# Order of the high and low parts in split float32 products, with an opening and an addition re-placed

## The chip, the cores and the metric

The kernel runs on one core of one Trainium2 chip. The metric is the device time of one execution in microseconds (us). TensorE (PE) multiplies matrices into PSUM, VectorE (DVE) and ScalarE (ACT) do the elementwise work, and transfers are issued from queues of SyncE (SP), ScalarE and GpSimd (POOL).

## The reference

One residual block of a streaming encoder on x of 2048 tokens by 1024 channels, all in float32:

```python
h = rmsnorm(x, norm_mix_pre)
proj = h @ w_in                      # 1024 -> pool 512 | glu 2*512 | gate_a 1024 | gate_b 1024
branch_a = pool_mixer(u_pool, pool_w, pool_scale, w_pool_out)
branch_b = conformer_conv(u_glu, conv_w, conv_b, ln_g, ln_b, w_conv_out)   # glu, width-31 causal conv, layernorm, silu
merged = sigmoid(g_a) * branch_a + sigmoid(g_b) * branch_b
x = x + rmsnorm(merged @ w_o, norm_mix_post)
h = rmsnorm(x, norm_mlp_pre)
f = square(relu(h @ w_up)) @ w_down   # 1024 -> 4096 -> 1024
x = x + rmsnorm(f, norm_mlp_post)
```

## The kernel before, in words

**Split operands.** TensorE gets each float32 operand as two reduced-precision parts: a high part, which ACT makes with a cast (lines 230 and 237), and a low part, which is the operand minus its high part and is made by DVE (line 131, in `split` and `split_w`). A product of operands a and b is hi*hi + hi*lo + lo*hi. So a weight tile is the pair `wh`, `wl`, and a token tile, called a cell, is a pair of tiles in the buffers `big`, `tr` or `fo`. A cell is 128 partitions by 1024: two slices of 128 channels, each for 512 tokens (`T`). Two cells make the 512-deep contraction of one product.

**One product.** `product` (line 301) multiplies one weight tile by two cells into a PSUM tile of 1024 columns, two halves q = 0 and 1. It has 24 matmuls of 128x512: for each half q, four slices k of the contraction (k = 0, 1 from the first cell, 2, 3 from the second), each with the three pairs of parts. `matmuls` (line 276) does the half q = 0 in full and then q = 1. The order within a half is that of `passes` (line 271): for k = 0, 1, 2 weight-high with cell-high and with cell-low; then the low weights of k = 0, 1, 2; then the three of k = 3. So the first cell's low part is read by the second matmul, the second cell's by the sixth, the low weights by the seventh. Calls that go straight to `matmuls` (the products named A, B, and wo of the first block of tokens) use the same order.

In the opening `product` hands over to `in_order` (line 312), which walks a list of (q, k, weight part, cell part). `STAIRS` (line 59) goes through one cell after the other, per cell high*high, then weight-high with cell-low, then weight-low with cell-high, four matmuls each, two for each half. `in_order` can also call a function when it has come to a given matmul (`inside`), so that what the function issues is placed there in the queues.

**Fast matrix multiplication.** Most of the products are those of a Strassen-like scheme with seven products for eight, numbered 1 to 7. An `Octet` (line 461) holds one such group: weights and cells are single tiles or sums and differences of tiles (`weight_parts`, line 339, `token_parts`), and three PSUM accumulators x, z, y take products 1, 6, 7, 4, then 2, then 5, 3. After each product `Octet.run` copies the accumulator out (`held`, line 475) or calls a `sink`, which adds a held copy to PSUM with DVE (`add`, line 128) and goes on. The accumulator can't be written by its next product before that.

**Stages.** w_in is used in groups glu, pool, ga and gb, for the first block of 1024 tokens, then for the second; then A, B and wo; then up (eight octets a block) and down. Beside the matmuls DVE runs the width-31 convolution (lines 1066 and 1070) as background work, in lanes that a call to `bg` after each product moves on by some instructions.

**Order of work.** A planner puts the program's instructions in each engine's queue from its own costs, by a priority that is the place in the program. `tc.high_priority(offset=n)` moves that priority n instructions forward; `URGENT` is 1500, `ahead[0]` is 45 at first and 260 later. `behind` puts background work after the marked instructions of the main line. Each queue runs in order. In the opening (`opening`, from line 1673 on) the order of DVE, ACT, PE and SP is instead written out: `fix`, an `InOrder`, ties each instruction to the one traced before it.

**The opening.** Its products 1 to 4 are glu of the octet o1, on tokens 0 to 511, products 5 and 6 are `o2.run(1)` and `o2.run(2)`. The next products come from `run_first` (line 603): four of o1 on tokens 512 to 1023 (products 7 to 10), then o2's 5, 6, 3, 7. Products 7 and 8 need the cells 8 and 3, made of x in tokens 512 to 1023. For these x is scaled by a gain per channel (`first_gain`, two ACT instructions of line 852) and by the root of the norm per token (a DVE product, line 134), with the root spread over partitions by PE (`n1.spread`, line 771) and copied to `r` by ACT (line 914). Before, this work is traced after product 5 (up to cell 8) and after product 6 (cell 3), `first_cell` (line 924) scales the cells.

Of the kernel before, what the change touches and what calls it, by code (L numbers as in the profile page):

```python
# [57 lines left out]
ORDER = (1, 2, 6, 5, 7, 3, 4)  # L58
STAIRS = tuple(
    (q, 2 * c + k, wp, xp)  # L60
    for c in (0, 1) for wp, xp in ((0, 0), (0, 1), (1, 0)) for q in (0, 1) for k in (0, 1)
)
COMING = tuple((q, k, 0, 0) for k in (0, 1) for q in (0, 1)) + ((0, 0, 0, 1), (1, 0, 0, 1))
# [13 lines left out]
def block_kernel(  # L77
# [49 lines left out]
    def add(o, a, b):  # L127
        return nc.vector.tensor_tensor(o, a, b, op=ALU.add)  # L128
# [21 lines left out]
    def mark(i):  # L150
        marks[i.ins.engine] = i.ins
        return i
# [147 lines left out]

    def product(ps, w, cells, start=True, stop=True):

        if in_opening:
            in_order(STAIRS, ps, w, cells, start, stop)
            return
        rhs = cell_rhs(cells)
        i = [matmuls(half_of(ps, q), w, 4 * q, rhs, start, stop) for q in (0, 1)]
        mark(i[1])

    in_opening = [True]  # L310

# [149 lines left out]
    class Octet:  # L461
# [18 lines left out]

        def run(self, i, then, bg):
            w, cells = self.w.pop(i, None) or self.weight(i), self.parts.need(i)
# [6 lines left out]
            ps = self.ps[acc]  # L489
            product(ps, w, cells, start=begins, stop=i in (2, 3, 4))  # L490
            flush()
# [27 lines left out]
    class Plain:  # L519
# [57 lines left out]
        def run(self, job, then, bg, inside=(None, None)):  # L577
# [7 lines left out]
            if t == 0:  # L585
                order = COMING if (m, k) == (0, 0) else STAIRS
                in_order(order, self.ps, w, cells, k == 0, k == 1, inside)
            else:
                product(self.ps, w, cells, start=k == 0, stop=k == 1)
            flush()  # L590
# [12 lines left out]
    def run_first(o, p, bg, dve):  # L603

        jobs = [(o, (m, 1, k)) for m in (0, 1) for k in (0, 1)]
        jobs += [(p, i) for i in (5, 6, 3, 7, 4)]
        for n, (u, i) in enumerate(jobs[:-1]):
            v, j = jobs[min(n + LOOK[n], len(jobs) - 1)]
            u.run(i, v.part(j) if v is o else j, bg)
            if n in NORM:  # L610
                dve.skip()
                o.norm(NORM.index(n))
                dve()
# [310 lines left out]
    def first_cell(c, t):  # L924
        x = x0[c, t]
        if t or c > 1:
            first_gain(c, t)
            mul(two(x), two(x), per_token(r0[t]))
            return x
# [624 lines left out]
    def mlp_up(b, parts):  # L1554
        def one(u):
# [117 lines left out]
    def opening():  # L1673
# [50 lines left out]
        with tc.high_priority(offset=URGENT):  # L1724
# [18 lines left out]
        fix()  # L1743
        o2.run(2, None, none)
        with tc.high_priority(offset=URGENT):
            o1.prepare(0, 1, 1)
            cells0(2, 1), cells0(3, 1)
            parts.need(3)
            o1.cast_behind = [
                i for i in nc.cur_bb.bb.instructions if i.engine == mybir.EngineType.Activation  # L1750
            ][-1]
        fix()
        o1.load_behind = fix.last[E.SP]
        dve.last.update(fix.last)
        in_opening.clear()

# [800 lines left out]
```

## Time and profile before

| | us |
|---|---|
| Median of 3 runs | 2153.82 (2153.32 to 2154.16) |
| The profiled execution | 2153.48 |
| Its span on the core | 2151.7 |
| TensorE busy | 2130.3 (99%) |
| VectorE busy | 1653.8 (77%) |
| ScalarE busy | 1047.7 (49%) |

A row of a timeline has the start, the length of the row, engine and line, the operation, its output and input by the program's names, the shapes and a count; a bracket is the idle time of the engine just before the row, with what ended it. Matmuls overlap in the pipeline, so the pace is read from starts and not from the length of one. A row of the view of windows has, per engine, busy us and number of instructions, and at the end the granted TensorE clock, the share of DMA and GB/s.

### The profile page before, as it was taken

The numbers are of one execution on the slowest core, as the hardware profiler recorded it, in microseconds if no ns is written. First come the engines' busy times: TensorE is split into PE (matmuls) and PEld (weight loads), VectorE is DVE, ScalarE is ACT, GpSimd is POOL, SyncE is SP. The second block draws the span as 40 slices with busy tenths as digits, with TensorE's granted clock in tenths as the row PEclk, the third lists the DMA queues.
The fourth block names the chain that finished last, engine by engine and source line by source line (L and its number), as shares of the span: only waits on it lengthen the run. The fifth ranks groups of instructions, "written<-read, shape, count | busy, mean of one in ns | idle before, by whom it ended". The sixth has DMA issues, their size and how long they took to land.

```text
span 2151.7 us, 25228 instructions
## 1 busy us (share of the span) xinstructions
PE 2130.3 (99%) x9549; PEld 1764.8 (82%) x9549; DVE 1653.8 (77%) x1621; ACT 1047.7 (49%) x1123; POOL 78.4 (4%) x143
## 2 busy tenths in 40 slices
PE   9999999999999999999999999999999999999998
PEld 7888888888888887888888888888888888888887
DVE  7898589997778869997868795667776657576975
ACT  8445454334443635445554684645663332234751
POOL 1000000000000000000000000000000000120002
PEclk9999999999999999999999999999999999999999
DMA  8789897768897787445697698677898997996977
GB/s 309 250 301 344 310 354 263 270 246 304 338 362 251 267 320 270 169 148 200 248 352 296 244 347 319 249 262 277 316 347 313 346 379 258 336 366 236 302 260 209
DMA packets 174506, 620.49 MB, mean 288 GB/s; under 512 B 19504, under 2 KB 21808, under 8 KB 174384
## 3 DMA queue, kind: packets, MB, share of 16 engines
q1 hardware_dynamic: 143456, 508.01, 64.8%
q0 software_dynamic: 17824, 64.07, 8.4%
q10 hardware_dynamic: 13104, 46.80, 5.5%
q8 instruction: 75, 1.23, 0.2%
q14 instruction: 47, 0.39, 0.0%
HBM read 408.99 MB, written 209.81 MB: 288 GB/s over the span
## 4 chain that ended last, share of the span: by engine, by line
PE 90%; DVE 5%; DMA 3%; ACT 1%; issue 1%; SPq 0%; DVEq 0%; ACTq 0%
PE up L280 24%; PE down L280 22%; PE wo L280 8%; PE ga L280 7%; PE gb L280 7%; PE glu L280 5%; PE rb L280 5%; PE A L280 4%; PE B L280 4%; PE pool L280 3%; DVE y L1070 1%; DVE big L131 1%; DVE tr L131 1%; PE glu L319 1%; DVE wl L131 1%
## 5 line engine op out<-in xcount | busy, mean ns | idle before, releaser
L280 PE MATMUL up<-big,wh 128*128 128x512 f32 x1792 | 481.3, 390 | 5.0 <-DVE tr L128 4.2
L280 PEld LDWEIGHTS up<-big,wh 128*128 128x128 f32 x1792 | 336.4, 188 | 76.2 <-issue 3.9
L237 ACT CAST wh<-wr 128x1024 fp32r<-128x1024 f32 x196 | 205.8, 1051 | 336.2 <-PE up L280 101.8
L1070 DVE SCALAR_TENSOR_TENSOR y<-v,cst,y 128x1024 f32<-128x1024 f32 x240 | 307.5, 1281 | 3.1
L280 PE MATMUL down<-big,wh 128*128 128x512 f32 x872 | 294.9, 389 | 0.0
L237 ACT CAST wh<-ws 128x1024 fp32r<-128x1024 f32 x128 | 134.6, 1052 | 302.3 <-PE up L280 91.6
L280 PE MATMUL up<-big,wl 128*128 128x512 f32 x896 | 277.0, 390 | 0.0
L280 PE MATMUL down<-big,wl 128*128 128x512 f32 x688 | 212.0, 389 | 0.0
L131 DVE TENSOR_TENSOR wl<-ws,wh 128x1024 fp32r<-128x1024 f32 x120 | 146.5, 1221 | 76.1 <-ACT wh L237 75.6
L280 PEld LDWEIGHTS up<-big,wl 128*128 128x128 f32 x896 | 168.7, 188 | 35.0
L280 PE MATMUL down<-tr,wh 128*128 128x512 f32 x504 | 196.2, 389 | 0.5 <-DVE tr L131 0.5
L280 PEld LDWEIGHTS down<-big,wh 128*128 128x128 f32 x872 | 163.6, 188 | 33.9
L131 DVE TENSOR_TENSOR wl<-wr,wh 128x1024 fp32r<-128x1024 f32 (+1 forms) x121 | 146.3, 1211 | 32.3 <-ACT wh L237 32.3
L131 DVE TENSOR_TENSOR big<-big,big 128x1024 fp32r<-128x1024 f32 (+1 forms) x108 | 129.9, 1221 | 41.0 <-ACT big L1205 19.6
L131 DVE TENSOR_TENSOR tr<-tr,big 128x1024 fp32r<-128x1024 f32 x94 | 112.6, 1221 | 56.5 <-ACT big L1975 43.8
L280 PEld LDWEIGHTS down<-big,wl 128*128 128x128 f32 x688 | 129.1, 188 | 26.8
L280 PE MATMUL wo<-big,wh 128*128 128x512 f32 x480 | 128.5, 389 | 0.0
L1975 ACT CAST big<-tr 128x1024 fp32r<-128x1024 f32 x70 | 72.0, 1048 | 102.1 <-DMA tr<-fd 79.9
L280 PE MATMUL gb<-big,wh 128*128 128x512 f32 x448 | 120.1, 389 | 0.0
L280 PE MATMUL ga<-big,wh 128*128 128x512 f32 x448 | 119.8, 389 | 0.0
L280 PEld LDWEIGHTS down<-tr,wh 128*128 128x128 f32 x504 | 94.6, 188 | 20.5 <-DVE tr L131 1.0
L280 PEld LDWEIGHTS wo<-big,wh 128*128 128x128 f32 x480 | 90.0, 188 | 18.5
(248 smaller groups left out, 3427.0 us busy)
## 6 DMA issues: line engine op xcount, KB each, us to landing
tr<-fd SPq DMA_DIRECT2D x98, 512.0 KB, 7.5
wl<-kept SPq DMA_DIRECT2D x85, 512.0 KB, 4.9
wr<-w_down SPq DMA_DIRECT2D x80, 512.0 KB, 7.5
kept<-wl SPq DMA_DIRECT2D x72, 512.0 KB, 6.2
wr<-w_up SPq DMA_DIRECT2D x64, 512.0 KB, 5.3
wr<-w_in SPq DMA_DIRECT2D x59, 512.0 KB, 5.2
fd<-tr ACTq DMA_DIRECT2D x54, 512.0 KB, 5.4
big<-fd SPq DMA_DIRECT2D x48, 512.0 KB, 6.4
```

Source lines behind the costliest of these rows:

```text
L131: return nc.vector.tensor_tensor(o, a, b, op=ALU.subtract)
L237: nc.scalar.copy(hi[:, :n], src[:, :n])
L280: i = nc.tensor.matmul(ps, w[wp][:, (at + k) * P : (at + k + 1) * P], rhs[k][xp], start=start and n == 0, stop=stop and n == len(order) - ...
L319: i = nc.tensor.matmul(half_of(ps, q), w[wp][:, (4 * q + k) * P : (4 * q + k + 1) * P], rhs[k][xp], start=start and q not in seen, stop=st ...
L1070: nc.vector.scalar_tensor_tensor(acc, v[:, k : k + TB], wk, acc, op0=ALU.mult, op1=ALU.add)
L1975: nc.scalar.copy(hi, t)
```

## The change

The products that go through `product` no longer do one half of PSUM after the other. They use `LATE_LOWS`: high*high of both cells, then low of the first cell, low weights of the first cell, low weights of the second cell, low of the second cell, four matmuls each, two for each half. Products 7 and 8 use `LOWS_BEHIND`, cell by cell, with low weights ahead of the low cell. The four last products by `product` in down (`END`) keep the order by halves.

In the opening, the second root's spread and the making of cells 8 are traced inside product 5, ahead of its last four matmuls (`second_half`), with one gain (of cell (1, 1)) moved from before the product to there and one (of (2, 1)) to the end of it; that of (3, 1) goes, since `first_cell` now scales this cell by gain and root at once. What was traced after product 6 is traced inside it at the same place (`last_cells`). In `run_first` the weights of the last product of o1 and of the first of o2 (number 5, a sum of two tiles) are prepared a product sooner. In up, the sink's addition gets the priority `URGENT`.

```diff
+def cellwise(*steps):
+    return tuple(
+        (q, 2 * c + k, wp, xp) for c, wp, xp in steps for q in (0, 1) for k in (0, 1)
+    )
+
+STAIRS = cellwise(*((c, *part) for c in (0, 1) for part in ((0, 0), (0, 1), (1, 0))))
+LOWS_BEHIND = cellwise(*((c, *part) for c in (0, 1) for part in ((0, 0), (1, 0), (0, 1))))
+LATE_LOWS = cellwise((0, 0, 0), (1, 0, 0), (0, 0, 1), (0, 1, 0), (1, 1, 0), (1, 0, 1))
...
-    def product(ps, w, cells, start=True, stop=True):
-        if in_opening:
-            in_order(STAIRS, ps, w, cells, start, stop)
+    def product(ps, w, cells, start=True, stop=True, order=LATE_LOWS):
+        if order is not None:
+            in_order(order, ps, w, cells, start, stop)
             return
...
-            product(ps, w, cells, start=begins, stop=i in (2, 3, 4))
+            if inside is not None:
+                in_order(STAIRS, ps, w, cells, begins, i in (2, 3, 4), inside)
+            else:
+                product(ps, w, cells, start=begins, stop=i in (2, 3, 4))
...
-                product(self.ps, w, cells, start=k == 0, stop=k == 1)
+                product(self.ps, w, cells, k == 0, k == 1, LATE_LOWS if m else LOWS_BEHIND)
...
             v, j = jobs[min(n + LOOK[n], len(jobs) - 1)]
+            if jobs[n + 1][0] is p and u is o:
+                u.prepare(*i)
+                p.prepare(5)
             u.run(i, v.part(j) if v is o else j, bg)
...
-        if t or c > 1:
+        if (c, t) not in ((0, 0), (1, 0), (3, 1)):
             first_gain(c, t)
...
                 if s is not None:
-                    mark(add(o, ps, s))
+                    with tc.high_priority(offset=URGENT):
+                        mark(add(o, ps, s))
...
             o2.prepare(2)
             first_gain(0, 1)
             parts.need(2)
-            first_gain(1, 1)
         fix()
-        o2.run(1, None, none)
-        with tc.high_priority(offset=URGENT):
-            n1.spread()
-            o1.prepare(0, 1, 0)
-            o1.get(1)
-            cells0(0, 1), cells0(1, 1)
-            first_gain(2, 1)
-            parts.need(8)
-            first_gain(3, 1)
+
+        def second_half():
+            with tc.high_priority(offset=URGENT):
+                n1.spread()
+                first_gain(1, 1)
+                o1.prepare(0, 1, 0)
+                o1.get(1)
+                cells0(0, 1), cells0(1, 1)
+                parts.need(8)
+                first_gain(2, 1)
+
+        def last_cells():
+            with tc.high_priority(offset=URGENT):
+                o1.prepare(0, 1, 1)
+                cells0(2, 1), cells0(3, 1)
+                parts.need(3)
...
+        o2.run(1, None, none, (20, second_half))
         fix()
-        o2.run(2, None, none)
-        with tc.high_priority(offset=URGENT):
-            o1.prepare(0, 1, 1)
-            cells0(2, 1), cells0(3, 1)
-            parts.need(3)
...
+        o2.run(2, None, none, (20, last_cells))
...
-        product(acc[0, b], weight_down(i, s, 0), end[n], start=n == 0, stop=s == LAST)
+        product(acc[0, b], weight_down(i, s, 0), end[n], n == 0, s == LAST, None)
```

More of the change, by code (lines that the diff above doesn't have):

```diff
@@ L58 @@
 ORDER = (1, 2, 6, 5, 7, 3, 4)
[L59 to L62, printed above, removed]
+def cellwise(*steps):
[5 more added lines that the diff above has]
+LATE_LOWS = cellwise((0, 0, 0), (1, 0, 0), (0, 0, 1), (0, 1, 0), (1, 1, 0), (1, 0, 1))
 COMING = tuple((q, k, 0, 0) for k in (0, 1) for q in (0, 1)) + ((0, 0, 0, 1), (1, 0, 0, 1))
@@ L308, in product @@
         mark(i[1])
-    in_opening = [True]
     def in_order(order, ps, w, cells, start, stop, inside=(None, None)):
@@ L479, in prepare, with run @@
             self.w[i] = self.weight(i)
-        def run(self, i, then, bg):
+        def run(self, i, then, bg, inside=None):
             w, cells = self.w.pop(i, None) or self.weight(i), self.parts.need(i)
@@ L1731, in opening @@
             parts.need(2)
-            first_gain(1, 1)
         fix()
-        o2.run(1, None, none)
-        with tc.high_priority(offset=URGENT):
-            n1.spread()
-            o1.prepare(0, 1, 0)
-            o1.get(1)
-            cells0(0, 1), cells0(1, 1)
-            first_gain(2, 1)
-            parts.need(8)
-            first_gain(3, 1)
-        fix()
-        o2.run(2, None, none)
-        with tc.high_priority(offset=URGENT):
-            o1.prepare(0, 1, 1)
-            cells0(2, 1), cells0(3, 1)
-            parts.need(3)
-            o1.cast_behind = [
-                i for i in nc.cur_bb.bb.instructions if i.engine == mybir.EngineType.Activation
-            ][-1]
+        def second_half():
[12 more added lines that the diff above has]
+                parts.need(3)
+                o1.cast_behind = [
+                    i for i in nc.cur_bb.bb.instructions if i.engine == E.Activation
+                ][-1]
+        o2.run(1, None, none, (20, second_half))
+        fix()
+        o2.run(2, None, none, (20, last_cells))
         fix()
@@ L1754, in opening @@
         dve.last.update(fix.last)
-        in_opening.clear()
     opening()
```

## The prediction

> **What bounds the kernel now.** I read the page first: span and share of each engine.
>
> ```profile
> span 2151.7 us, 25228 instructions
> PE 2130.3 (99%) x9549; PEld 1764.8 (82%) x9549; DVE 1653.8 (77%) x1621; ACT 1047.7 (49%) x1123; POOL 78.4 (4%) x143
> ```
>
> TensorE is busy for all but 21.4 us, and the change takes away no matmul. So it can win only what TensorE stands still for or runs slowly. The view of waits by engine, for PE, comes next (us in total, times, longest):
>
> ```profile
> PE up L280 <- DVE tr L128: 4.2, 2, 3.5
> PE glu L280 <- DVE big L131: 1.6, 2, 0.8
> ```
>
> Line 128 is the addition that empties PSUM, line 131 a low part. The rest of the view is single waits of 1 us and less. Now the timeline of PE gives each wait its place. First the pace without a wait, in both orders of a product:
>
> ```profile
> 28.04 1.07 PE L319 MATMUL glu<-big,wl 128*128 128x512 f32 x4
> 36.20 1.07 PE L319 MATMUL glu<-big,wl 128*128 128x512 f32 x4
> 69.08 1.52 PE L280 MATMUL glu<-big,wh 128*128 128x512 f32 x6
> 90.84 1.52 PE L280 MATMUL pool<-big,wh 128*128 128x512 f32 x6
> ```
>
> From 28.04 to 36.20 lie 36 matmuls of the opening's order, which changes the weights at each matmul and the half of PSUM at every second: 8.16/36 = 0.2267 us. From 69.08 to 90.84 lie four products by halves, 96 matmuls: 21.76/96 = 0.2267 us. A product of 24 is 5.44 us.
>
> **Part 1, the opening (products 5 to 8).** Product 7 follows product 6, product 8 follows at the row of 51.43:
>
> ```profile
> 42.57 1.07 PE L319 MATMUL glu<-big,wl 128*128 128x512 f32 x4
> 44.56 0.50 PE L280 MATMUL glu<-big,wh 128*128 128x512 f32 x1 [0.92 <-ACT big L230]
> 45.81 1.64 PE L280 MATMUL glu<-big,wh 128*128 128x512 f32 x5 [0.76 <-DVE big L131]
> 51.43 0.39 PE L280 MATMUL glu<-big,wh 128*128 128x512 f32 x1
> 52.62 1.63 PE L280 MATMUL glu<-big,wh 128*128 128x512 f32 x5 [0.80 <-DVE big L131]
> ```
>
> Product 7 was due at 42.57 + 4 x 0.2267 = 43.48 and began 1.08 late. Its second matmul was due at 44.79 and came 1.02 late; product 8's second was due at 51.66 and came 0.96 late. Together 3.06 us. What they wait for, on ACT and DVE:
>
> ```profile
> 37.73 1.04 ACT L230 CAST big<-big 128x1024 fp32r<-128x1024 f32 x1
> 38.67 1.33 ACT L852 ACTIVATE big<-big,cst 128x512 f32<-128x512 f32 x2
> 40.80 0.58 ACT L914 COPY r<-rb 128x512 f32<-128x512 f32 x1
> 43.47 1.99 ACT L230 CAST big<-big 128x1024 fp32r<-128x1024 f32 x2
> ```
>
> ```profile
> 36.00 0.16 DVE L131 TENSOR_TENSOR sq<-sy,sp 128x4 fp32r<-128x4 f32 x1
> 39.49 1.22 DVE L131 TENSOR_TENSOR big<-big,big 128x1024 fp32r<-128x1024 f32 x1
> 41.41 2.36 DVE L134 TENSOR_TENSOR big<-big,r 128x1024 f32<-128x1024 f32 x2 [0.71 <-ACT r L914]
> 46.81 1.22 DVE L128 TENSOR_TENSOR tr<-glu,tr 128x1024 f32<-128x1024 f32 x1
> ```
>
> The second root is spread after product 5. The change spreads it four matmuls (0.91 us) sooner, from 36.20; its input ends at 36.16, which leaves 0.04. ACT's copy into r then follows the cast of 37.73, at 38.7 in place of 40.80, since the gain of 38.67 and the held copy now stand behind it. DVE goes on at the end of its low part, 40.63, in place of 41.41: products by r end at 41.8 and 42.9. On ACT come, behind the copy, one gain (40.4), the cast of the weight (41.4), the high casts (42.8 and 43.9) without the second gain between; on DVE the low parts, at 44.0 and 45.2. Product 7 needs its first high part at 43.48, the first low part at its ninth matmul, 45.3, the second high part at 46.2: no wait, with 0.7, 1.3 and 2.3 in hand.
>
> Product 8 is due at 48.92. ACT has a gain, the held copy and a cast first (1.3 + 1 + 1, near 47.1), then the high parts (48.1, 49.1); DVE two products and low parts (49.3, 50.5). Cell (3,1) trades its gain on ACT for two half instructions on DVE. The first high part has 0.8 in hand. This is the thinnest cover of the part; if a gain more stood ahead of it, product 8 would wait 0.5. The sink's addition of product 6 (now 46.81) moves to about 51.7, behind these; product 9, which needs its PSUM buffer, is due at 54.36, so 2.7 hide that. Also moved: two raw weight loads and two loads of kept low parts, past a flush's store on SP.
>
> ```profile
> 40.08 0.32 SPq L137 DMA_DIRECT2D wl<-kept  x1
> 64.98 1.22 DVE L128 TENSOR_TENSOR ws<-wr,wr 128x1024 f32<-128x1024 f32 x1
> 66.28 1.05 ACT L237 CAST wh<-ws 128x1024 fp32r<-128x1024 f32 x1 [3.20 <-DVE ws L128]
> ```
>
> Product 8's low weights are asked for at 40.08, and product 8 now wants them at its fifth matmul, 49.8: 9.7 us of cover. The weight sum of 64.98 belongs to the product that begins at 69.08, which becomes due at 66.02. Its cast ends at 67.33, 1.3 late if nothing moved. The change prepares it a product (5.44 us) sooner; I cost it at nothing. Sum of the part: -3.06, bounds -3.06 and, if the gain meets that weight and product 8's cast, -1.3.
>
> **Part 2, up's additions.**
>
> ```profile
> 809.08 1.66 PE L280 MATMUL up<-big,wh 128*128 128x512 f32 x6 [0.75 <-DVE tr L128]
> 836.41 1.52 PE L280 MATMUL up<-big,wh 128*128 128x512 f32 x6
> 841.62 0.39 PE L280 MATMUL up<-big,wl 128*128 128x512 f32 x1
> 845.51 1.83 PE L280 MATMUL up<-big,wh 128*128 128x512 f32 x6 [3.50 <-DVE tr L128]
> 851.31 0.85 PE L280 MATMUL up<-big,wl 128*128 128x512 f32 x3
> ```
>
> ```profile
> 845.50:852.50 7.00, 6.99 (x24) 5.59 (x25) 7.00 (x7) 3.03 (x3) 0.00 (x0) 0.76 0.77 303
> ```
>
> ```profile
> 836.08 1.28 DVE L1070 SCALAR_TENSOR_TENSOR y<-v,cst,y 128x1024 f32<-128x1024 f32 x1
> 837.27 1.22 DVE L131 TENSOR_TENSOR tr<-big,tr 128x1024 f32<-128x1024 f32 x1
> 840.86 1.06 ACT L230 CAST big<-tr 128x1024 fp32r<-128x1024 f32 x1
> 841.88 2.35 DVE L131 TENSOR_TENSOR big<-tr,big 128x1024 fp32r<-128x1024 f32 x2
> 844.15 1.22 DVE L128 TENSOR_TENSOR tr<-up,tr 128x1024 f32<-128x1024 f32 x1
> ```
>
> The product due at 841.62 + 0.227 = 841.85 writes the PSUM that the addition of 844.15 reads. It begins at 845.51: 3.66 lost. In the same place the granted clock is 0.76 on average (in the row of the window 845.50 to 852.50 the third number from the right, ahead of DMA share and GB/s), and the 18 matmuls from 845.51 to 851.31 take 5.80 in place of 4.08: 1.72 more. The addition's input was there at 836.41 and a little; DVE meanwhile did convolution and, at the last, the low parts of the very product that waits. Putting the addition ahead alone would only exchange it for those low parts. With the new order of the product it pays: low parts are wanted from the ninth matmul.
>
> The estimate: the addition after the instruction of 836.08, at 837.3 to 838.4; all behind it 1.14 later. The second high cast (now 840.86 to 841.92) ends at 843.0, wanted at 841.85 + 0.91 = 842.76; the first low part ends at 844.2, wanted at 843.9. Some 0.5 of waiting is left of 3.66. Bounds: 0 (the planner still puts it behind the low parts) and 3.66. DVE worked without a break from one addition to the next, and the instructions between are traced near it, so the priority decides the place and not readiness: I take 3.2.
>
> The clock: the short waits of 0.75 and 0.92 have no slow matmuls behind them, this one of 3.50 has. So with the wait gone the 1.72 goes too. [...]
>
> Sum: -4.9 (-3.2 - 1.7), bounds 0 and -5.38. The wait of 809.08 (0.91 with its restart) I leave: its addition stood in the queue behind a weight sum that waited for a load, and priority helps only if that sum isn't picked first. Bound -0.91.
>
> **Part 3, low parts last everywhere.**
>
> ```profile
> 1263.31 1.29 PE L280 MATMUL up<-big,wh 128*128 128x512 f32 x5
> 1265.39 0.50 PE L280 MATMUL up<-big,wh 128*128 128x512 f32 x1 [0.79 <-DVE big L131]
> 1981.77 0.39 PE L280 MATMUL down<-big,wh 128*128 128x512 f32 x1
> 1982.70 0.50 PE L280 MATMUL down<-tr,wh 128*128 128x512 f32 x1 [0.54 <-DVE tr L131]
> ```
>
> Both stop at the sixth matmul, the second cell's low part: 1265.39 - 1264.44 = 0.95 and 1982.70 - 1982.00 = 0.70. In the new order that operand comes at matmul 21, 3.4 us later, so both waits go; of the second I count 0.3 and not 0.70, since the matmuls behind it want DVE's low parts too and may wait in its place. Sum -1.25, bounds 0 and -1.65. High parts are wanted no sooner than before (second cell at matmul 5 both times), the second half of PSUM at matmul 3 in place of 13, but one instruction frees both halves. A low weight is let go four matmuls sooner, a high one a matmul later (0.23); a cast runs two products ahead of its use, which hides it. The products of A and B don't pass through `product`, so their waits stay.
>
> **Sum.** -3.06 - 4.9 - 1.25 = -9.2. The profiled execution took 2153.48 (its span and 1.8 around it), 0.34 under the median of 2153.82; the loss is the same in both, so 2153.8 - 9.2 = 2144.6.
>
> **Rivals.**
> - *The addition does not move* (the planner's place for it was readiness): the 5.4 at 841.62 stay. For: additions wait behind work for the same products. Against: the unbroken queue. 2153.8 - 4.3 = 2149.5. Chance 0.14.
> - *The opening only shifts its wait* (0.04 at the spread, 0.8 at product 8 are thin): 2 to 3.06 us come back: 2146.6 to 2147.7. Chance 0.10.
> - *A new wait elsewhere.* Each queue between the written-out stages is planned anew, and one draw like 841.62 costs 5.4. For: DVE is dense from 790 to 850. Against: every operand moved is wanted later. 2150.0. Chance 0.13.
> - *Slower: the pace.* 319 products, 7656 matmuls, change to halves of PSUM in turn; each ns more is 7.7 us, so above 1.2 ns it eats the gain, and at 2.5 ns the time is 2154 - 9 + 19 = 2164. Against: 0.2267 in both orders, uncertain by 0.02/36 = 0.6 ns, at most 4.6 us either way. [...] Chance 0.05.
> - The rest, 0.03, is small mishaps without a gain. The forecast keeps 0.55.
>
> **How the numbers follow.** 0.2% is 4.3 us, about what a measurement of this kernel can tell from no change: below 2149.5 counts as faster. The forecast and the shifted opening lie there, and half of the unmoved addition: 0.55 + 0.10 + 0.07 = 0.72. Within: 0.07 + 0.13 + 0.01 = 0.21. Slower 0.07. The range: all bounds together give 3.06 + 0.91 + 5.38 + 1.65 = 11.0, so 2142.8, with 0.4 for the spread of runs 2142.4; above, up to the new wait's 2150.0.
>
> **What would show it.** Right: no wait at products 7 and 8; in up's second half-dozen products additions right behind a product's end, no 0.5 clock near 845; the low-part waits near 1264 and 1982 gone; 24 matmuls in 5.44 us still. Wrong: an addition still behind two low parts; a wait for ACT's high cast in its place; a pace of 0.228 or more; a PE wait of several us that before doesn't have.

## The result

The kernel after takes 2140.51 us, the median of six runs from 2139.65 to 2142.01, against 2153.95 for the kernel before in the same comparison (six runs, 2150.66 to 2154.72). The ratio is 0.994, interval 0.9928 to 0.9953. The change is faster by 13.4 us where 9.2 was forecast, and the time lies 1.9 us below the range. The profiled execution took 2140.78 (before: 2153.48).

The page and the whole answer on PE's waits, after:

```profile
span 2139.0 us, 25137 instructions
PE 2125.6 (99%) x9549; PEld 1764.6 (82%) x9549; DVE 1652.6 (77%) x1622; ACT 1047.4 (49%) x1121; POOL 78.3 (4%) x143
```

```profile
PE rb L664 <- POOL inv_d L203: 1.0, 1, 1.0
PE glu L324 <- DVE wh L576: 0.7, 1, 0.7
PE up L324 <- ACT tr L480: 0.5, 1, 0.5
PE rb L770 <- DVE sy L731: 0.5, 1, 0.5
```

DVE, ACT and POOL are busy as long as before, within 1.2 us. PE is busy 4.7 us less with as many matmuls. Before, the 18 matmuls from 845.51 took 5.80 us in place of 4.08, and the one at 44.56, behind a wait, has a row of 0.50 where the one at 51.43 has 0.39; fewer of both would fit the 4.7, but it was not taken apart. The line of 4.2 us for additions is no longer there, nor any line for a low part. (The change shifts the lines: 324 is the matmul of the new orders, 287 that of a product by halves, 135 the addition, 138 the subtraction that makes a low part, 244 the cast of a high weight, 237 that of a high cell, 480 the held copy, 1585 the squared ReLU's first step.)

Products 7 and 8 of the opening, on PE's timeline: no row has a bracket, that is, a wait, and each starts where the one before leaves off.

```profile
42.80 1.07 PE L324 MATMUL glu<-big,wl 128*128 128x512 f32 x4
43.71 1.07 PE L324 MATMUL glu<-big,wh 128*128 128x512 f32 x4
44.62 1.07 PE L324 MATMUL glu<-big,wl 128*128 128x512 f32 x4
45.52 1.98 PE L324 MATMUL glu<-big,wh 128*128 128x512 f32 x8
47.34 1.07 PE L324 MATMUL glu<-big,wl 128*128 128x512 f32 x4
48.24 1.98 PE L324 MATMUL glu<-big,wh 128*128 128x512 f32 x8
```

In up, where 5.4 us were lost, DVE now has the addition in front of the two low parts (832.34, then 833.48), and PE runs product after product:

```profile
831.21 1.22 DVE L138 TENSOR_TENSOR tr<-big,tr 128x1024 f32<-128x1024 f32 x1
832.34 1.22 DVE L135 TENSOR_TENSOR tr<-up,tr 128x1024 f32<-128x1024 f32 x1
833.48 2.35 DVE L138 TENSOR_TENSOR big<-tr,big 128x1024 fp32r<-128x1024 f32 x2
```

```profile
835.18 3.79 PE L324 MATMUL up<-big,wh 128*128 128x512 f32 x16
840.62 3.79 PE L324 MATMUL up<-big,wh 128*128 128x512 f32 x16
846.06 3.79 PE L324 MATMUL up<-big,wh 128*128 128x512 f32 x16
```

```profile
832.50:848.50 16.00, 16.00 (x72) 13.27 (x71) 16.00 (x14) 9.57 (x10) 0.00 (x0) 1.00 0.71 248
```

From 835.18 to 840.62 and on to 846.06 are 5.44 us each: the pace is what it was. The granted clock in this window is 1.00 (before, behind the wait: 0.76). Both waits for low parts are gone too; near the first there is another, for a held copy on ACT:

```profile
1261.68 1.07 PE L324 MATMUL up<-big,wh 128*128 128x512 f32 x4
1263.23 3.02 PE L324 MATMUL up<-big,wh 128*128 128x512 f32 x12 [0.48 <-ACT tr L480]
...
1977.10 1.98 PE L324 MATMUL down<-big,wl 128*128 128x512 f32 x8
1978.91 1.07 PE L324 MATMUL down<-tr,wh 128*128 128x512 f32 x4
1979.82 0.39 PE L324 MATMUL down<-big,wh 128*128 128x512 f32 x1
```

To weigh kernels against each other I summed, over PE's matmuls after the first 30 us, all that lies from one start to the next above the pace, where it is over 0.15 us. Before it is 13.3: 3.07 in the opening, 0.34 at the pool's products near 385, 0.77 and 0.32 in B, 0.91 at 809, 5.24 at 842, 0.95 at 1264, 0.70 at 1982, 0.38 at 2015, 0.62 at the end. After it is 1.55: 0.29, 0.64 and the same 0.62. So the waits that the forecast left in place went as well. The rest of the 12.7 us between the two profiled executions, 0.95, is 1.5 less in steps under 0.15 us and 0.5 more behind the last matmul; the first 30 us are alike to 0.1. That is an account of where, not of why.

### The profile page after: what moved, and what is told of

Its sections match the earlier page's. It is cut to its first block, busy times and chain, and to the rows that moved or that the text cites. A ratio compares the mean times of both kernels' runs of the same rounds, so it can differ in the third digit from the quotient of the medians.

```text
span 2139.0 us, 25137 instructions
## 1 busy us (share of the span) xinstructions
PE 2125.6 (99%) x9549; PEld 1764.6 (82%) x9549; DVE 1652.6 (77%) x1622; ACT 1047.4 (49%) x1121; POOL 78.3 (4%) x143
## 4 chain that ended last, share of the span: by engine, by line
PE 89%; DVE 5%; DMA 3%; issue 2%; ACT 1%; POOL 0%; SPq 0%; POOLq 0%; DVEq 0%; ACTq 0%
PE up L324 28%; PE down L324 21%; PE gb L324 7%; PE ga L324 6%; PE wo L287 4%; PE A L287 4%; PE rb L324 4%; PE B L287 4%; PE wo L324 4%; PE glu L324 4%; PE pool L324 2%; DMA big<-x1d 1%; DVE wl L138 1%; DVE y L1081 1%; DMA wr<-w_in 1%
## 5 line engine op out<-in xcount | busy, mean ns | idle before, releaser
L324 PE MATMUL up<-big,wh 128*128 128x512 f32 x1792 | 427.4, 390 | 0.5 <-ACT tr L480 0.5
L324 PE MATMUL up<-big,wl 128*128 128x512 f32 x896 | 221.3, 389 | 0.0
L324 PE MATMUL down<-big,wh 128*128 128x512 f32 x840 | 204.7, 389 | 0.0
L324 PEld LDWEIGHTS down<-big,wh 128*128 128x128 f32 x840 | 157.5, 188 | 32.7
L324 PE MATMUL down<-big,wl 128*128 128x512 f32 x656 | 162.2, 389 | 0.0
L324 PE MATMUL down<-tr,wh 128*128 128x512 f32 x472 | 126.2, 389 | 0.0
L324 PE MATMUL glu<-big,wh 128*128 128x512 f32 x464 | 113.0, 390 | 0.7 <-DVE wh L576 0.7
L324 PE MATMUL ga<-big,wh 128*128 128x512 f32 x448 | 108.0, 390 | 0.1
L324 PE MATMUL gb<-big,wh 128*128 128x512 f32 x448 | 107.5, 389 | 0.0
L324 PEld LDWEIGHTS glu<-big,wh 128*128 128x128 f32 x464 | 86.8, 188 | 19.4 <-ACT big L863 1.3
```

Source lines behind the costliest of these rows:

```text
L324: i = nc.tensor.matmul(half_of(ps, q), w[wp][:, (4 * q + k) * P : (4 * q + k + 1) * P], rhs[k][xp], start=start and q not in seen, stop=st ...
```

## The experiments

Times are medians, gains are against the kernel before in the same comparison, and "the loss" is the total of PE's losses as above, in the profiled execution; "weight sum" is the addition of w_up's parts on DVE that waits for its load near 808. In an order of a product, "wanted at 16" means that 16 matmuls precede the first that reads an operand, "free at 24" that the 24th is the last to read it.

### How much the executions of one kernel differ

**again**: the kernel before, unchanged. **after_again**: the kernel after, unchanged.

> The kernel before, unchanged, for a second profile. Theory 1 (each wait is built into the order of the queues): the same waits of PE at the same places, each within 0.1 us: 3.06 us at products 7 and 8 of the opening, 0.77 and 0.32 in B, 0.91 and 5.38 in up's first block, 0.95 near 1264, 0.70 near 1982. Theory 2 (the waits for DMA landings, in B above all, are chance of one execution): B's two waits and the one near 809 differ by more than 0.3 us from the first profile, the others stay.

2152.49 in the profiled execution. B's two waits and the one at 809 are absent, and the loss is 11.06 and not 13.3; the opening, 1264, 1982 and 2015 are the same to 0.04. At 842 it is 4.1 and not 5.2, and at the pool's products 0.83 and not 0.34. So of the waits that disappeared, 2.0 us (809 and B) come and go in the kernel before by itself.

> The changed kernel, unchanged, for a second profile and a second measurement. Theory 1 (the waits gone by the change are gone in every execution; those for landings, in B and near 809, come and go with either kernel): gain 11.5 to 12.5 us against the kernel before on the same chip, no wait over 1 us after the opening, none in up's first block. Rival (the first result paired a slow draw of before with a good one of after): gain 9 to 10.

2139.95 (2139.77 to 2141.73), a gain of 12.4, ratio 0.9948, 0.9935 to 0.996; the loss is 2.15, with 0.57 in B.

### Each part by itself

**order_alone**: the orders of the products without the rest.

```diff
-        product(self.ps, w, cells, start=k == 0, stop=k == 1)
+        product(self.ps, w, cells, k == 0, k == 1, LATE_LOWS if m else LOWS_BEHIND)
...
+    def product(ps, w, cells, start=True, stop=True, order=LATE_LOWS):
```

> The kernel before with the new order of parts alone (low parts last; products 7 and 8 cell by cell with low cells last); the opening's work, the weight sum and up's addition as before. Theory 1 (low weights are let go sooner, so loads behind them in SP's queue start sooner and B's waits go too): the waits for low parts go, 1.02 + 0.96 in the opening, 0.95 and 0.70 later, and B's 1.09; the addition of 844 stays behind the low parts, so 5.4 stays. Gain 4.7 us. Theory 2 (B's waits vanished by chance or by another part): gain 3.6, with 0.7 and more of waiting in B. If the planner moves the addition because of the order, the gain is 9 to 10.

2143.76, a gain of 8.8; ratio 0.9962, 0.9949 to 0.9974. This is the miss. Some 0.8 of it are waits in the opening (2.26 of loss are left there, 3.07 before), which the prediction counted in part 1; the other 8.0 are more than six times what the prediction gave to this part. Its profiled execution happened to be its slowest (2148.16) and still has a wait of 2.49 in up.

**urgent_alone**: only the priority of up's additions.

```diff
-                    mark(add(o, ps, s))
+                    with tc.high_priority(offset=URGENT):
+                        mark(add(o, ps, s))
```

> The kernel before with only the higher priority of up's addition. Theory 1 (priority decides its place): the addition near 844 moves ahead of the low parts, PE then waits for these in its place, 2 to 2.5 us, and the clock stays full: gain 3 to 3.5, plus 0.9 if the addition near 808 moves too. Rival (readiness in the plan decides): no change, 0 to 0.9. B's waits stay in both.

2150.68, a gain of 1.9; ratio 0.9988, 0.9979 to 0.9997. The addition near 842 moves, and 1.14 of loss stays there. That place thus loses 4.1 us less, more than the time gains: in this execution PE loses 1.13 near 598, where the kernel before has nothing. **no_urgent**, the kernel after with these two lines undone:

> The changed kernel without the higher priority of up's addition. Theory 1 (with the new order the planner already puts the addition near 808 ahead of the weight sum that waits for its load, so DVE doesn't fall behind, and the addition near 842 is in time even behind the low parts): within 1 us of the changed kernel, gain 11 to 12. Rival (the priority is what cures the wait near 842): wait of 2.6 to 3 there and 1.3 to 1.7 of slow clock, gain 7.5 to 8.5.

2141.41 (2141.2 to 2142.3), so by the medians the priority is worth 1.5 in the kernel after; the ranges of the two overlap. The one wait that comes back, on DVE and PE:

```profile
832.99 2.35 DVE L138 TENSOR_TENSOR big<-tr,big 128x1024 fp32r<-128x1024 f32 x2
835.26 1.21 DVE L135 TENSOR_TENSOR tr<-up,tr 128x1024 f32<-128x1024 f32 x1
```

```profile
834.70 1.07 PE L324 MATMUL up<-big,wh 128*128 128x512 f32 x4
836.62 2.98 PE L324 MATMUL up<-big,wh 128*128 128x512 f32 x12 [0.85 <-DVE tr L135]
```

The addition stands behind the two low parts again, as before the change, but the next product comes only 1.0 late and not 3.66. Here the order of the parts has taken away the larger share of this wait. It does not always: order_alone, with the same order and no priority either, has its wait of 2.49 at this place. Its weight sum started 16.39 us after up's first matmul, the latest of all, where this one started at 12.94, and its addition near 842 stands 1.6 us further back.

**opening_alone**: the re-placed opening with the weight sum of 65 prepared sooner, all other products by halves.

```diff
-        o2.run(1, None, none)
+        o2.run(1, None, none, (20, second_half))
...
-        o2.run(2, None, none)
+        o2.run(2, None, none, (20, last_cells))
```

> The kernel before with the opening's re-placed work and the sooner weight sum, all products in the old order by halves (5 and 6 as before). Theory 1: the late start of product 7 (1.08) goes; its second and sixth matmul still wait some 0.3 each for low parts, product 8 not: gain 2.4 us, all waits after the opening as before, B's too. Rival (later stages shift with the opening because DMA and DVE there are the limit): gain under 1.5.

2149.73, a gain of 2.9; ratio 0.9985, 0.9976 to 0.9994. The waits of products 7 and 8 are gone (0.53 of loss is left in the opening); the waits at 842, 1264, 1982 and 2015 stay. **no_opening** is the kernel after with the old opening and without the weight sum that is prepared sooner (at 65), **no_sum** the kernel after without the three lines of that alone.

```diff
-            if jobs[n + 1][0] is p and u is o:
-                u.prepare(*i)
-                p.prepare(5)
```

> The changed kernel with the opening's work and the weight sum as before: order of parts (products 7 and 8 too) and priority alone. If the opening's waits for high parts (1.2 and 0.9 with the order alone) are all that the re-placing saves: 2 us less gain than the changed kernel, 9.5 to 10.5. If it also decides later stages: 3 us or more less.

2143.45, 3.5 above the kernel after in another comparison; products 7 and 8 wait for their high casts again, 2.1 together. The rest of the 3.5 has no one place. With the old opening nobody waits at 65.

> The changed kernel without the sooner preparation of the weight sum after the opening. If the prediction's step is right, the product that begins near 66 waits for its weight's cast, up to 1.3 us, and the gain is 1 us less; if DVE and ACT have the sum in time anyway, no difference over 0.5.

2141.84, 1.9 above the kernel after in another comparison. One wait of more than 1 us comes back, and it is the one whose price the prediction worked out as 1.3:

```profile
64.57 1.07 PE L324 MATMUL glu<-big,wh 128*128 128x512 f32 x4
66.65 3.04 PE L324 MATMUL glu<-big,wh 128*128 128x512 f32 x12 [1.02 <-ACT wh L244]
```

66.65 - 64.57 - 4 x 0.2267 = 1.17.

**by_halves**: the opening and the priority, all other products in the old order.

```diff
-    def product(ps, w, cells, start=True, stop=True, order=LATE_LOWS):
+    def product(ps, w, cells, start=True, stop=True, order=None):
```

> The changed kernel with all products but the opening's 5 and 6 in the old order by halves, so the opening's work, the weight sum and the addition's priority alone. Theory 1 (the parts add up: 2.9 of the opening and 1.9 of the priority, the order has the rest): gain 4.5 to 5.5, waits for low parts near 1260 and 1978 as before. Rival (parts need each other): gain under 3.5.

2146.34, a gain of 6.1; ratio 0.9976, 0.9967 to 0.9985. Put on top of this, the order is worth another 6.4. The waits at 1264 and 1982 stay here to 0.01, so these two do belong to the order.

### What in the order does it

The order of the kernel after differs from the old one in several ways at once. Most of these runs change LATE_LOWS alone and keep the rest of the change.

**low_weights_last**: low parts late as well, but the low weights last.

```diff
-LATE_LOWS = cellwise((0, 0, 0), (1, 0, 0), (0, 0, 1), (0, 1, 0), (1, 1, 0), (1, 0, 1))
+LATE_LOWS = cellwise((0, 0, 0), (1, 0, 0), (0, 0, 1), (1, 0, 1), (0, 1, 0), (1, 1, 0))
```

> The changed kernel with the low weights read last in each product (high by high of both cells, low cells, then low weights): low parts are still late, but a low weight's buffer comes free at matmul 24 as before the change, and not at 20. Theory 1 (what counts is that low parts are wanted late): gain as the changed kernel's within 1 us. Rival (the buffer that comes free sooner starts the loads behind it sooner): 1 to 3 us less gain, the addition near 808 behind the weight sum again.

2153.33, ratio 1.0007, 0.9998 to 1.0016: all of the gain is gone, that of the opening and the additions too, though every low part is wanted later than by halves. So "low parts last" can't be the whole of it. What this order has besides is a high weight that is free at 16.

**swapped**: only the last two steps change places; the high weight is free at 20, the low weight at 24.

```diff
+LATE_LOWS = cellwise((0, 0, 0), (1, 0, 0), (0, 0, 1), (0, 1, 0), (1, 0, 1), (1, 1, 0))
```

> The changed kernel with the last two steps of each product swapped: the second cell's low part at matmul 17, its low weights at 21. A low weight's buffer is then free at matmul 24 and the high one's at 20, where the change has 20 and 24. Low parts are as late as in the change, within four matmuls. Theory A (which of a weight's two buffers comes free first decides how the planner and the queues place casts, low parts and loads): 5 us or more of the gain go, waits in B and up come back. Theory B (late wanting of low parts is what gains; the loss of the order with low weights last has another cause, its sixteen matmuls of low cells ahead): within 1.5 us of the changed kernel.

2149.61 (2145.49 to 2152.68), ratio 0.9984, 0.9975 to 0.9993: nine of the twelve us are lost by the exchange of eight matmuls. The loss is 7.89.

**weights_soon**: the low weight is wanted at 4 and free at 16, the low parts of the cells come last, the high weight is free at 24.

```diff
+LATE_LOWS = cellwise((0, 0, 0), (0, 1, 0), (1, 0, 0), (1, 1, 0), (0, 0, 1), (1, 0, 1))
```

> The changed kernel with low weights of the first cell at matmul 5, of the second at 13, and low cells last (17 and 21): a low weight's buffer is free at matmul 16, a high one's at 24. Low weights are not wanted late any more. Theory A (release order): the gain stays, 11 to 12.5. Theory B (late wanting): waits for low weights of 0.5 to 2 us come in up, gain 9 to 11.

2146.89, ratio 0.9973, 0.9962 to 0.9983. Up is nearly as in the kernel after (1.02 for 0.64 near 1263); the loss is in down (3.83 after 1300), mostly for casts of weights.

From these I formed two theories, that the low weight has to go free early (A1) or that the high weight has to go free last (A2), and tested them with small moves. **tail_swap** is the kernel before with one exchange; **edge_low** and **edge_high** move one and seven matmuls of the kernel after.

```diff
-        return order + [(0, n - 1, 0), (0, n - 1, 1), (1, n - 1, 0)]
+        return order + [(0, n - 1, 0), (1, n - 1, 0), (0, n - 1, 1)]
```

```diff
+LATE_LOWS = LATE_LOWS[:19] + LATE_LOWS[20:] + LATE_LOWS[19:20]
```

```diff
+LATE_LOWS = LATE_LOWS[:16] + LATE_LOWS[20:23] + LATE_LOWS[16:20] + LATE_LOWS[23:]
```

> The kernel before (every product still in its old order, half by half, nothing re-placed) with only the last two matmuls of each half changed places, so that the last matmul of a product reads a high weight (24) and the one ahead of it the last low weight (23). Theory A2 (the high weight's buffer goes free last, so the next high cast can't stand ahead of the copy that empties PSUM): most of what the order is worth beyond the two late castings, a gain of 4 to 7 us against the kernel before (2152.4), about 2147, with the addition near 808 ahead of the sum of the weight that is awaited. Theory A1 (a low weight's buffer goes free four or more matmuls sooner) and my first account (low parts wanted later): nothing, within 1 us of the kernel before.

2151.05, a gain of 2.6 by the medians with a ratio of 0.9992, 0.9983 to 1.0001, an interval that includes no gain. A2 foresaw the place of the addition rightly (11.1 us after up's first matmul, ahead of the weight sum; before 15.96), and it is worth little: the losses at 842 fall to 1.44, but PE waits 1.0 more at the pool's products (half of that in the kernel before's second execution too) and 1.0 more at 598, and in the opening the granted clock falls (0.58 from 46 to 50, last section).

> The kernel after with one matmul moved in each product of late lows: the last of the four by a low weight of the second cell goes from place 20 to place 24, so that a low weight is read last and the high weight at 23. A2: most of the order's larger part is lost, 2145 to 2150 with the addition near 808 behind the awaited sum, as in the kernel that swapped the last two steps (2149.61). A1: lost as well, in like measure. The first account (low parts wanted later): within 1 us of the kernel after (2140).

2141.24, ratio 0.9946, 0.9934 to 0.9959. The addition near 808 (here at 803) is behind the weight sum again and costs 0.79, and nearly all of the gain stays. A2 in its sharp form falls: reading the high weight at the very last is worth about 1 us. A1 falls with it, since the low weight goes free at 24 here.

> The kernel after with its last four low-weight matmuls and three of the four by the second cell's low parts exchanged: the low weight is read up to place 23, the high weight last, at 24. A2: as the kernel after, 2140 to 2142, with the addition near 808 ahead of the awaited sum. A1 (what counts is that the low weight goes free four matmuls before the end): 5 us or more slower than the kernel after, 2145 or over.

2144.24, ratio 0.996, 0.9947 to 0.9972: a loss of some 3 to 4 us that A2 doesn't explain, and less than A1 foresaw.

Two readings were left for the swapped kernel: the second cell's low part is wanted at 16 and not at 20, or the high weight goes free at 20 and not at 24. **want_16** and **want_16_low_last** want that low part at 16, with the high weight free at 24 and at 23.

```diff
+LATE_LOWS = LATE_LOWS[:16] + LATE_LOWS[20:21] + LATE_LOWS[16:20] + LATE_LOWS[21:]
```

```diff
+LATE_LOWS = LATE_LOWS[:16] + LATE_LOWS[20:21] + LATE_LOWS[16:19] + LATE_LOWS[21:] + LATE_LOWS[19:20]
```

> The kernel after with one matmul moved in each product of late lows: the first of the four by the second cell's low part goes from place 20 to place 16. That low part is wanted as early as in the kernel that swapped the last two steps (2149.61), but the high weight is still read last (24) and the low weight up to 21. Theory W (what counts is how late the low parts are wanted): 2143.5 to 2149, towards the swapped kernel. Theory R (what counts is when the high weight's buffer goes free: at 16 2153.33, at 20 2149.61, at 23 2141.24, at 24 2139.95): within 1.5 us of the kernel after, 2139.5 to 2141.5.

2140.56, ratio 0.9943, 0.9931 to 0.9956: no loss.

> The kernel that wants the second cell's low part at place 16, with one low-weight matmul moved to place 24 as well, so that the low weight goes free last, as in the swapped kernel, and the high weight at 23. From the swapped kernel it differs only in that the high weight's buffer goes free at 23 and not at 20. R: as the kernel with one low-weight matmul last (2141.24), 2140.5 to 2142.5. W: 2143.5 or over. If a low weight that goes free last and a low part that is wanted at 16 together make the swapped kernel slow: 2147 to 2150.

2141.79, ratio 0.995, 0.9936 to 0.9964. It differs from the swapped kernel by the three low-part matmuls that move from in front of the low weight's behind three of them. The high weight goes free three matmuls later (23 for 20, 0.68 us), and 7.8 us lie between the two, with intervals that don't touch. In all these orders the last matmul by the high weight is also the last by the second cell's low part, so the times alone can't tell which of the two buffers counts. One place where the swapped kernel goes wrong, at 1066, points to the weight's; it is 1.31 of its 7.89 us of loss, and most of its other waits end with an addition or a low part on DVE. On ACT and PE:

```profile
1060.48 1.06 ACT L244 CAST wh<-ws 128x1024 fp32r<-128x1024 f32 x1 [1.28 <-PE up L324]
1065.92 1.05 ACT L244 CAST wh<-wr 128x1024 fp32r<-128x1024 f32 x1 [4.38 <-PE up L324]
1066.87 1.02 ACT L1585 ACTIVATE tr<-up 128x1024 f32<-128x1024 f32 x1
```

```profile
1061.19 2.88 PE L324 MATMUL up<-big,wh 128*128 128x512 f32 x12
...
1065.72 1.07 PE L324 MATMUL up<-big,wl 128*128 128x512 f32 x4
1067.94 3.01 PE L324 MATMUL up<-big,wh 128*128 128x512 f32 x12 [1.15 <-ACT tr L1585]
```

A product ends as the next begins at 1061.19. The ReLU that empties its PSUM has its input from there on, but two casts stand ahead of it, and the second waits 4.38 us for the next product to let go of a high weight. In the kernel shown next the same ReLU runs right at its product's end. Here it starts 5.7 us later, and the product due at 1065.72 + 0.91 = 1066.63 starts 1.31 late. That place in the kernel that frees the high weight at 23 (its lines are one higher):

```profile
1058.56 1.06 ACT L245 CAST wh<-ws 128x1024 fp32r<-128x1024 f32 x1 [1.97 <-PE up L325]
1059.52 1.01 ACT L1586 ACTIVATE tr<-up 128x1024 f32<-128x1024 f32 x1
```

One cast, then the ReLU at once: nobody waits. In the swapped kernel ACT stood 4.38 us at the cast with the ReLU's input at hand and did not take the ReLU first.

**after_ab**, for a version that beats both: the same idea in the products that the change left by halves (A, B, the output's and the last slabs).

```diff
-        order = [(0, k, p) for k in range(n - 1) for p in (0, 1)]
-        order += [(1, k, 0) for k in range(n - 1)]
-        return order + [(0, n - 1, 0), (0, n - 1, 1), (1, n - 1, 0)]
+        order = [(0, k, 0) for k in range(n)] + [(0, k, 1) for k in range(n // 2)]
+        return order + [(1, k, 0) for k in range(n)] + [(0, k, 1) for k in range(n // 2, n)]
```

> The kernel after with the same idea in the products that the change left half by half (A, B, the output projection and the last slabs): high parts by high parts, half of the low cells, the low weights, the other low cells, so that a high weight is read last there too. If the two small waits of B that stayed in a second run of the kernel after (0.57 and 0.67, of which B has the first) are the same sort, it gains 0.3 to 1 us, 2139 to 2139.7; if the waits that come in other stages take it back, nothing, within 0.5 us of the kernel after.

2140.96, ratio 0.9943, 0.993 to 0.9957: the loss falls to 1.26, but no gain over the kernel after can be measured. Of what was run, nothing beats the kernel after.

## Why the prediction came out short

**What was right.** The opening: -3.06 forecast, 2.9 by itself and 3.5 when it is taken away, both with the earlier weight sum of 65. That one: 1.3 if it didn't move, 1.17 in its wait. The pace: 0.2267 us in both orders, so the slower rival is out. The two waits for low parts at 1264 and 1982 go with the order and with nothing else, though near 1264 a wait for ACT takes back 0.64 of 0.95. The granted clock behind 842 is 1.00 with the wait gone, where it was 0.76.

**The step that failed** is part 3, "Sum -1.25, bounds 0 and -1.65". The order by itself brought 8.8 us, and on top of the rest 6.4, of which 0.8 and 0.5 lie in the opening. I had priced the order by the two waits that end with a low part, as if only an instruction that PE visibly waits for could matter. But the order sets two things for the whole queue of the other engines:

- *When low parts are wanted.* Before, the 5.4 us at 842 ended with an addition, not a low part; the addition stood behind two low parts that the product wanted at its second and sixth matmul. Without the priority, but with the new order, that place loses 1.0 in no_urgent and 2.65 in order_alone. Part 2 gave all of it to the priority, -4.9; the priority by itself is worth 1.9, and 1.5 last. From by_halves to edge_low (high weight free at 23, low weight at 24 in both) lie 5.1 us by the times and 6.3 by the gains. That low parts are wanted late is the chief difference between the two, not the only one: the halves of PSUM alternate in edge_low, and products 7 and 8 have another order (0.5).
- *When weights' buffers go free.* "A high one a matmul later (0.23); a cast runs two products ahead of its use, which hides it" counted the delay of the cast and not its place in the queue. With the high weight free at 16 the time is 2153.33, at 20 2149.61, at 23 2141.24 and 2141.79, at 24 2139.95 and 2140.56. Of the orders with the rest of the change that free it at 24, two take longer: weights_soon, which wants the low weight at 4, and edge_high (below). That the step from 20 to 23 is this and not the low weight or the time at which the low part is wanted is shown by want_16 and want_16_low_last; that it is the weight's buffer and not the second cell's low part, which goes free with it, was not tested apart and rests on the rows at 1066. At 16 the low weight is wanted later, at 16, and the second cell's low part sooner, at 12.

**Luck in the sum.** Part 2 was put some 3 us too high and part 3 5 to 7 too low. That the sum missed by no more than 4.2 us is in part that these two errors cancel.

**The wait of 809.** "Its addition stood in the queue behind a weight sum that waited for a load, and priority helps only if that sum isn't picked first." Without the priority it goes too: what moves the addition ahead is the high weight's being read last. Held copy and cast on ACT, before and then after:

```profile
797.26 1.06 ACT L237 CAST wh<-wr 128x1024 fp32r<-128x1024 f32 x1 [1.26 <-PE up L280]
798.22 1.01 ACT L475 COPY tr<-up 128x1024 f32<-128x1024 f32 x1
```

```profile
792.77 1.02 ACT L480 COPY tr<-up 128x1024 f32<-128x1024 f32 x1 [3.01 <-PE up L324]
793.68 1.05 ACT L244 CAST wh<-wr 128x1024 fp32r<-128x1024 f32 x1
```

and on DVE addition and weight sum:

```profile
806.66 1.23 DVE L128 TENSOR_TENSOR ws<-wr,wr 128x1024 f32<-128x1024 f32 x1 [6.59 <-DMA wr<-w_up]
807.80 1.22 DVE L128 TENSOR_TENSOR tr<-up,tr 128x1024 f32<-128x1024 f32 x1
```

```profile
798.21 1.23 DVE L135 TENSOR_TENSOR tr<-up,tr 128x1024 f32<-128x1024 f32 x1 [2.22 <-PE up L324]
...
800.12 1.23 DVE L135 TENSOR_TENSOR ws<-wr,wr 128x1024 f32<-128x1024 f32 x1
```

In all eighteen different kernels this place follows the order: in the ten that read a high weight at 24 (tail_swap and no_urgent among them) the addition starts 11.08 us after up's first matmul, ahead of the weight sum; in the eight others it starts behind it, at 13.4 to 15.96. The weight sum starts 12.3 to 16.4 us after up's first matmul, by execution, when its load has landed. With the addition behind it, that delay goes on to PE when it is long: the two traces whose addition starts at 15.84 and 15.96 lose 0.79 and 0.91 there, the others, up to 14.72, nothing. With the addition ahead of it, none loses anything there. This fits the narrower spread (2139.65 to 2142.01, against 2150.66 to 2154.72), but that the spread comes from here was not tested.

**A and B.** "Their waits stay" can't be judged by one trace: 0.77 and 0.32 in the kernel before, none in its second execution; none in the kernel after, 0.57 in its second. My low end of the range took the waits of one execution as fixed. It had 809's 0.91 in its bounds, but left out B's 1.1, which the kernel before has in some executions only.

**What stays open.** edge_high, with the low weight free at 23 and the low part wanted at 16, takes 2144.24; want_16, with the low weight free at 21, takes 2140.56, and the intervals overlap by 0.0009. Whether the low weight costs something there, or the execution, isn't settled. Nor did I follow why a load of up lands up to 4 us later in one execution than in another. The planner's costs weren't printed: that it places casts by the matmul that frees their buffer is read from the queues in the traces.

## What to carry to other kernels

The order of matmuls inside a product sets when every operand is wanted and when every buffer goes free; where a planner writes the other engines' queues from these times, a change of order is a change of all queues, and it isn't priced by the waits that name its operands. Look at what stands in the queue ahead of the instruction that PE waits for: here it was a low part, or a cast waiting for a buffer, in front of the addition or ReLU that empties PSUM. Take the waits of at least two executions before calling a wait fixed.

## What the runs showed of the hardware

The prediction took it that waits of 0.75 and 0.92 us keep the clock and 3.50 doesn't. In these runs a wait's length alone set no such bound. In up, order_alone stood still for 2.49 us, low_weights_last for 2.49 and the second execution of the kernel before (the run called again) for 2.64:

```profile
843.49 2.78 PE L324 MATMUL up<-big,wh 128*128 128x512 f32 x11 [2.49 <-DVE tr L135]
```

```profile
868.98 0.50 PE L324 MATMUL up<-big,wh 128*128 128x512 f32 x1 [2.49 <-DVE tr L135]
```

```profile
844.27 2.90 PE L280 MATMUL up<-big,wh 128*128 128x512 f32 x6 [2.64 <-DVE tr L128]
```

The first runs on at full pace (11 matmuls in 2.78); the third needs 2.90 for six. The granted clock of a window behind each, in this order, is 1.00, 0.76 and 0.77:

```profile
840.50:847.50 7.00, 4.51 (x21) 3.40 (x20) 7.00 (x7) 3.14 (x3) 0.00 (x0) 1.00 0.66 215
```

```profile
868.00:875.00 7.00, 6.02 (x19) 4.81 (x20) 7.00 (x7) 4.41 (x5) 0.00 (x0) 0.76 0.37 149
```

```profile
844.00:851.00 7.00, 6.73 (x24) 5.49 (x25) 7.00 (x7) 3.13 (x3) 0.00 (x0) 0.77 0.79 314
```

And in tail_swap the clock fell at two waits of the opening about as short as those of the kernel before:

```profile
44.86 0.50 PE L280 MATMUL glu<-big,wh 128*128 128x512 f32 x1 [1.00 <-ACT big L230]
46.12 2.09 PE L280 MATMUL glu<-big,wh 128*128 128x512 f32 x5 [0.76 <-DVE big L131]
```

Five matmuls take 2.09 here and 1.64 in the kernel before. The granted clock is 0.58 in this window of tail_swap, and 1.00 through the opening's waits of the kernel before:

```profile
46.00:50.00 4.00, 3.88 (x10) 3.03 (x11) 4.00 (x5) 2.62 (x4) 0.00 (x0) 0.58 0.38 134
```

```profile
44.00:54.00 10.00, 7.88 (x30) 5.45 (x31) 9.46 (x9) 8.63 (x11) 0.00 (x0) 1.00 0.52 163
```

Behind the wait of 3.50 in the kernel before, the granted clock stays at 1.00 for 1.25 us of matmuls, from 845.51 to 846.76, is 0.50 for the next 3.41, and then 1.00 again:

```profile
835.00:846.76 11.76, 8.26 (x37) 6.52 (x37) 11.76 (x12) 6.53 (x7) 0.00 (x0) 1.00 0.52 177
846.76:850.17 3.41, 3.41 (x10) 2.64 (x9) 3.41 (x4) 1.80 (x2) 0.00 (x0) 0.50 0.55 221
850.17:860.00 9.83, 9.83 (x45) 8.12 (x44) 7.70 (x7) 5.76 (x6) 0.00 (x0) 1.00 0.98 355
```

The drops here came at waits of 3.50, 2.64 and 2.49, and at 1.00 with 0.76 close behind; none came at another of 2.49, nor at 0.92 with 0.76 close behind. What sets waits of one length apart was not shown.
